# Adaptive modulation: a vector-matrix product moved from TensorE to VectorE, with one TensorE sum over partitions

## The chip, the cores and the metric

One core of a Trainium2 chip runs the whole program in one launch. The metric is the device time of a run in microseconds, as the median of several runs.

## The reference, cut to what matters

Two blocks of a network follow each other over 256 tokens of width 1024, in float32. Block one has two layers, each a mixer, a cross attention and a gated FFN (hidden width 2816). Block two is conditioned on a vector `c`: one product gives six vectors of 1024 that shift, scale and gate it.

```python
mod = jax.nn.silu(c) @ w_ada[l] + b_ada[l]        # (1, 1024) @ (1024, 6144)
shift1, scale1, gate1, shift2, scale2, gate2 = jnp.split(mod, 6, axis=-1)
h = modulate(rms_norm_2(x, norm_pre_mix[l]), shift1, scale1)
...
x = x + gate1[:, None, :] * rms_norm_2(mix @ w_out[l], norm_post_mix[l])
h2 = modulate(rms_norm_2(x, norm_pre_ffn[l]), shift2, scale2)
y = expert_choice_ffn(h2, w_router[l], w_gate[l], w_up[l], w_down[l])   # 16 experts, hidden 2816
x = x + gate2[:, None, :] * rms_norm_2(y, norm_post_ffn[l])
```

The modulation depends on `c` alone, so its 25 MB weight can be worked on at any time before block two. The 16 experts' weights are 554 MB.

## The kernel before, in words

**Weights of block one.** Dense weights come from memory in units of 1 MB (tile `raw`, three buffers). Each unit is used in two halves of 128 x 1024, and each half is split into a high float32r part by ScalarE (`wh`, L206) and the rest by VectorE (`wl`, L207). There are five buffers for halves, and a next half is split as soon as the products of an earlier one have freed its place. Every product is three TensorE products (L249 to L251).

**The second layer's FFN** (`ffn`, L886) runs through 11 groups g of 256 hidden columns, and a round here is one g: the gate's product, the up product, and the down product of group g-1. After the gate's product comes a tanh on ScalarE and `fth` on VectorE (L903); after the up product comes another `fth` (L913), which is split into `dH` on ScalarE (L289) and `dL` on VectorE (L290). The program calls `between()` after the gate's and after the down product, and each call puts in one unit of a list of fills.

**The modulation** (`ada_unit`, L987) is that list in the second layer: 24 units A0 to A23. Each has 1 MB of `w_ada` (tile `adw`, two buffers, all 1024 rows by 256 columns). TensorE multiplies it in eight products of 128x256 with `crep`, which holds silu(c) repeated 32 times (L1001); four partial sums lie 32 partitions apart in PSUM. They are split into high and low parts (`adsb`, L1007 and L1008), and one unit later two products with the selecting matrix `sel` add the four (L1015, tile `ae`); VectorE adds bias and gain (L1018 to L1021). A0 and A1 are put ahead of the transposes of the norm before the FFN (`bound`, L1073), A2 behind them, A3 to A23 into the FFN. The last sum is flushed in the first norm of block two (L1277).

**Queues.** The order is written out by hand and every engine works in the program's order. All weights are loaded through SyncE's one queue. A load whose place is still in use waits there, and every load behind it waits too.

**Memory of the experts' stage.** The pool `work` of all that comes before is released and the pool of the experts is laid over the same addresses, so an expert's load waits until the last reader of what lay in its slot has finished. From the lowest address on, `work` holds:

```python
decay = tile_(work, (P, 4, S), "decay")       # 4096 bytes of a partition
causal = tile_(work, (P, P), "causal")        # 512
cos = tile_(work, (P, 2, 32), "cos")          # 256
sin = tile_(work, (P, 2, 32), "sin")          # 256
rep8 = tile_(work, (8, P), "rep8")            # 512
identr = tile_(work, (P, 8), "identr", F32R)  # 32
crep = tile_(work, (P, KC, 32), "crep")       # 1024
hH = tile_(work, (P, KC, S), "hH", F32R)      # 8192
hL = tile_(work, (P, KC, S), "hL", F32R)      # 8192
```

Next come two tiles of 4096 bytes with the tag `gain`. Gains of the norms use them, and in the routing, the last stage before the experts, the normalised rows `h2T` (L1495), which the router's product `plg` reads (L1029). The experts have 14 slots of 2816 x 4 = 11264 bytes, placed by a list:

```python
SLOTS_AT = [1, 2, 11, 5, 3, 7, 8, 9, 12, 13, "y", "hid", "hT", "ds", "sT", "fs", 10, 0, 4, 6]
```

So slot 1 has bytes 0 to 11264 of the pool and slot 2 bytes 11264 to 22528. The first load of expert 0 goes to slot 0, the second to slot 1, the third to slot 2, and so on (`feed` in `experts`, L1622, issues at L1632 and L1635). The 15th load waits until TensorE has used the first one's slot.

Of the kernel before, what the change touches and what calls it, by code (L numbers as in the profile page):

```python
# [8 lines left out]
F32 = mybir.dt.float32  # L9
# [22 lines left out]
def shape_constants():  # L32
    """Constants that depend on shapes and positions in an array alone."""
# [16 lines left out]
    sel = np.zeros((P, P), np.float32)  # L50
    sel[0::32, :] = 1.0
    c["k_sel"] = sel
# [12 lines left out]
def log1p_coefficients(degree=9, n=200):  # L65
    """The polynomial of log(1 + y) / y through its Chebyshev nodes on [0, 1]."""
    t = np.cos(np.pi * (np.arange(n) + 0.5) / n)
    y = (t + 1) / 2
    cheb = np.polynomial.chebyshev.chebfit(t, np.log1p(y) / y, degree)
    poly = np.polynomial.Polynomial(np.polynomial.chebyshev.cheb2poly(cheb))  # L70
    return [float(v) for v in poly(np.polynomial.Polynomial([-1.0, 2.0])).coef]
# [6 lines left out]
def tile_kernel(ctx: ExitStack, tc: tile.TileContext, I, out, stop=None):  # L78
# [22 lines left out]
    # what is used up first lies lowest: the experts' weights take its place  # L101
# [6 lines left out]
    crep = tile_(work, (P, KC, 32), "crep")  # L108
# [6 lines left out]
    # the parts of what goes into a second projection; the memory holds other  # L115
    # things before
# [9 lines left out]
    # ---------------------------------------------------------------- steps  # L126
# [40 lines left out]
    def run_program():  # L167
# [7 lines left out]
        def feed():  # L175
            # the last weight has a place of its own, so that no load behind it waits
# [87 lines left out]
    def proj_n(W, o, aH, aL, t):  # L264
        """o[token, column] of a half of the tokens."""
# [26 lines left out]
    # ---------------------------------------------------------------- norms  # L292
# [39 lines left out]
    def pre_norm_b(t, xg, dg, oH, oL):  # L332
        """oH + oL = transpose of norm(src) * gain for a half of the tokens."""
# [10 lines left out]
    def post_norm_a(t, acc, gain):  # L344
# [3 lines left out]
        # one bank's squares beside the other's products  # L348
# [18 lines left out]
    # ------------------------------------------------------------ once only  # L367
# [17 lines left out]
    def prepare():  # L385
# [17 lines left out]
        # 2 softplus(-lam), and -4  # L403
# [10 lines left out]
        nc.vector.tensor_scalar(ct, ct, 0.5, None, op0=OP.mult)  # L414
        nc.vector.tensor_copy(crep, ct[:, :, None].to_broadcast([P, KC, 32]))

    # ----------------------------------------------------- memory's keys, values
# [44 lines left out]
    def mixer(l, fill, also=(lambda: None,) * 3):  # L462
# [39 lines left out]
        def fox_spread():  # L502
            # -8 times the sums, and rows of zeros below them
# [314 lines left out]
    def gelu2(o, src, pool, shape, key):  # L818
        """o = 2 gelu(src), its tanh form; src in PSUM."""
# [8 lines left out]
    # --------------------------------------------------------- cross attention  # L828
# [59 lines left out]
    # ------------------------------------------------------------------- ffn  # L888
    def ffn(l, between):
# [50 lines left out]
    # ------------------------------------------------- block two: modulation  # L940
    B = {}

    def ada_open():
# [17 lines left out]
        B["sel"] = p.tile([P, P], F32R, name="sel", tag="sel", bufs=1)  # L961
        raw = p.tile([P, 256], F32, name="selraw", tag="adb", bufs=2)[:, :P]
        nc.sync.dma_start(raw, I["k_sel"])
        ada_rest.append(lambda: nc.scalar.copy(B["sel"], raw))
# [5 lines left out]
    ADA = [(j, u) for j in (1, 0, 2, 4, 3, 5) for u in range(4)]  # L970
    ada_w = {}

    def ada_load(i):
        if i < len(ADA):
            j, u = ADA[i]
            src, shp = cols(I["w_ada_2"][0], j * D + 256 * u)
# [775 lines left out]
```

## Time and profile before

| what | us |
|---|---|
| median of 3 runs | 2388.23 |
| range of the runs | 2387.13 to 2389.67 |
| profiled execution: its span, first to last instruction (the page lists no other time of it) | 2385.8 |
| busy: TensorE / VectorE / ScalarE | 1815.9 / 747.7 / 542.2 |
| data moved | 747.16 MB, mean 313 GB/s |

The span is 2.4 us shorter than the median of the runs. Engines are named PE (TensorE products), PEld (its weight loads), DVE (VectorE), ACT (ScalarE), POOL (GpSimd) and SP (SyncE). Busy shares of the whole span mix stages that have different limits: the first 1085 us or so are dense work on TensorE, the rest is the experts. So the stages are read apart.

### The profile page before, as it was taken

The page shows a single profiled execution, that of the slowest core. Times are in us where ns is not written, and L with a number is a line of the kernel's source. Part 1 is how long each engine was busy: PE and PEld are TensorE (multiplying, and loading weights), DVE is VectorE, ACT ScalarE, POOL GpSimd, SP SyncE. Part 2 cuts the span into 40 slices and gives each one's busy share as a digit, 9 for nine tenths or more (in the row PEclk, how much of TensorE's full clock was granted, in tenths as well). Part 3 has the DMA queues.
Part 4 walks back from the last instruction along what each step waited for, and adds up shares of the span by engine and source line. Part 5 has one row for each costly group of instructions (what it writes and reads, how often), then busy time and mean ns, then how long its engine had stood idle before and what let it go on. Part 6 is the DMA issues. An engine that isn't in the chain of part 4 may idle for free.

```text
span 2385.8 us, 30667 instructions
## 1 busy us (share of the span) xinstructions
PE 1815.9 (76%) x13172; PEld 1152.7 (48%) x13172; DVE 747.7 (31%) x1147; ACT 542.2 (23%) x882; POOL 54.8 (2%) x96
## 2 busy tenths in 40 slices
PE   7999999999989999979556656655655665565565
PEld 7889899988878888964111111111111111111111
DVE  5774555557656555651000000000000000000001
ACT  4554444445444333531000000000000000000000
POOL 0010000000000000020000000000000000000000
PEclk9999999999999999979999899989999999999999
DMA  6344555453568886569999999999999999999997
GB/s 218 124 166 161 176 184 188 142 172 123 186 204 287 279 279 196 181 235 365 419 421 417 416 422 419 417 418 422 417 416 420 419 417 417 422 418 416 420 421 287
DMA packets 244423, 747.16 MB, mean 313 GB/s; under 512 B 21024, under 2 KB 151728, under 8 KB 211520
## 3 DMA queue, kind: packets, MB, share of 16 engines
q1 hardware_dynamic: 241696, 744.40, 80.7%
q8 instruction: 103, 1.69, 0.3%
q10 hardware_dynamic: 2592, 0.81, 0.1%
q14 instruction: 32, 0.26, 0.0%
HBM read 743.99 MB, written 1.05 MB: 312 GB/s over the span
## 4 chain that ended last, share of the span: by engine, by line
DMA 52%; PE 37%; DVE 5%; ACT 2%; POOL 1%; issue 1%; SPq 1%; ACTq 0%; POOLq 0%; DVEq 0%
DMA ed<-in_w_down_dram 18%; DMA eu<-in_w_up_dram 18%; DMA eg<-in_w_gate_dram 15%; PE fu L249 2%; PE fu L251 2%; PE fu L250 2%; PE fg L249 2%; PE fg L251 2%; PE fg L250 2%; PE facc L251 2%; PE facc L250 2%; PE facc L249 2%; DVE wl L207 1%; PE ad L1001 1%; PE pd L1686 1%
## 5 line engine op out<-in xcount | busy, mean ns | idle before, releaser
L207 DVE TENSOR_TENSOR wl<-raw,wh 128x1024 fp32r<-128x1024 f32 (+1 forms) x284 | 341.5, 1216 | 228.9 <-ACT wh L206 228.2
L1686 PE MATMUL pd<-ed,hT 128*32 128x512 f32 x1408 | 319.5, 617 | 93.6 <-DMA ed<-in_w_down_dram 89.0
L1659 PE MATMUL pu<-eu,xsT 128*32 128x384 f32 (+1 forms) x2048 | 205.3, 481 | 199.3 <-DMA eu<-in_w_up_dram 199.3
L1659 PE MATMUL pg<-eg,xsT 128*32 128x384 f32 (+1 forms) x2048 | 201.1, 479 | 190.8 <-DMA eg<-in_w_gate_dram 190.8
L206 ACT CAST wh<-raw 128x1024 fp32r<-128x1024 f32 (+1 forms) x284 | 292.1, 1042 | 226.7 <-PE fg L250 44.2
L1664 DVE SCALAR_TENSOR_TENSOR hid<-hid,pg 128x384 f32<-128x384 f32 (+2 forms) x48 | 19.8, 413 | 720.9 <-ACT hid L1663 720.9
L1686 PEld LDWEIGHTS pd<-ed,hT 128*32 128x32 f32 x1408 | 69.6, 111 | 331.4 <-DMA ed<-in_w_down_dram 165.2
L1659 PEld LDWEIGHTS pu<-eu,xsT 128*32 128x32 f32 x2048 | 62.1, 111 | 330.6 <-DMA eu<-in_w_up_dram 276.5
L1659 PEld LDWEIGHTS pg<-eg,xsT 128*32 128x32 f32 x2048 | 56.1, 111 | 332.2 <-DMA eg<-in_w_gate_dram 266.2
L1663 ACT ACTIVATE hid<-pg 128x384 f32<-128x384 f32 (+2 forms) x48 | 18.3, 381 | 829.9 <-PE pg L1659 773.3
L1698 DVE TENSOR_TENSOR y<-y,po 128x512 f32<-128x512 f32 x60 | 41.3, 688 | 409.9 <-PE po L1693 409.9
L249 PE MATMUL fu<-hH,wh 128*128 128x256 f32 x352 | 100.3, 285 | 0.0
L251 PE MATMUL fu<-hH,wl 128*128 128x256 f32 x352 | 100.3, 285 | 0.0
L250 PE MATMUL fu<-hL,wh 128*128 128x256 f32 x352 | 100.2, 285 | 0.0
L249 PE MATMUL fg<-hH,wh 128*128 128x256 f32 x352 | 99.6, 283 | 0.0
L1688 ACT COPY ds<-pd 128x512 f32<-128x512 f32 x16 | 9.4, 585 | 396.8 <-PE pd L1686 396.8
L250 PE MATMUL fg<-hL,wh 128*128 128x256 f32 x352 | 99.5, 283 | 0.0
L251 PE MATMUL fg<-hH,wl 128*128 128x256 f32 x352 | 99.5, 283 | 0.0
L251 PE MATMUL facc<-wh,dL 128*128 128x512 f32 x176 | 69.3, 393 | 0.0
L250 PE MATMUL facc<-wl,dH 128*128 128x512 f32 x176 | 68.9, 391 | 0.0
L249 PE MATMUL facc<-wh,dH 128*128 128x512 f32 x176 | 68.6, 390 | 0.0
L249 PEld LDWEIGHTS fu<-hH,wh 128*128 128x128 f32 x352 | 68.0, 193 | 0.0
(614 smaller groups left out, 3210.3 us busy)
## 6 DMA issues: line engine op xcount, KB each, us to landing
eg<-in_w_gate_dram SPq DMA_DIRECT2D x128, 1408.0 KB, 26.7
eu<-in_w_up_dram SPq DMA_DIRECT2D x128, 1408.0 KB, 27.1
ed<-in_w_down_dram SPq DMA_DIRECT2D x175, 1024.0 KB, 19.0
raw<-in_w_in_dram SPq DMA_DIRECT2D x31, 1024.0 KB, 5.5
adw<-in_w_ada_dram SPq DMA_DIRECT2D x24, 1024.0 KB, 8.6
raw<-in_w_gate_dram SPq DMA_DIRECT2D x22, 1024.0 KB, 5.2
raw<-in_w_up_dram SPq DMA_DIRECT2D x22, 1024.0 KB, 5.2
raw<-in_w_down_dram SPq DMA_DIRECT2D x22, 1024.0 KB, 5.2
```

What stands on the lines that cost most here:

```text
L206: nc.scalar.copy(h, v)
L207: nc.vector.tensor_tensor(l, v, h.bitcast(F32), op=OP.subtract)
L249: nc.tensor.matmul(o, aH, bH, start=first, stop=False)
L250: nc.tensor.matmul(o, aH, bL, start=False, stop=False)
L251: nc.tensor.matmul(o, aL, bH, start=False, stop=last)
L1001: nc.tensor.matmul(o[b:b + 32, :], crep[:, k, :], W[:, k, :], start=k < 4, stop=k > 3)
L1659: nc.tensor.matmul(pg[n][32 * j:32 * j + 32, b, :m * P].rearrange("p (c f) -> p c f", f=P), B["xsT"][:, k, 32 * e:32 * e + 32], w[:, c0:c0 ...
L1663: nc.scalar.activation(d, pg["g"][:np_, b, c0:c1], AF.Tanh, scale=0.5)
L1664: nc.vector.scalar_tensor_tensor(d, d, 1.0, pg["g"][:np_, b, c0:c1], op0=OP.add, op1=OP.mult)
L1686: nc.tensor.matmul(pd[n][32 * j:32 * j + 32, :], hT[:, i, 32 * j:32 * j + 32], w[:, a * D + n * 512:a * D + n * 512 + 512], start=i == 0, ...
L1688: nc.scalar.copy(ds_[:, :512], pd[0])
L1698: nc.vector.tensor_tensor(yb, yb, po, op=OP.add)
```

## The change

- `crep` becomes `csil`, one value of silu(c) a row: 32 bytes of a partition where there were 1024. All that lies above it in `work` moves down by 992 bytes.
- A unit is now half of the rows (512) by 512 columns, still 1 MB. VectorE multiplies each chunk of 128 rows by its silu(c) and adds it to an accumulator `ada` of 128x512: four instructions a unit, the very first of a pair a `tensor_scalar`, the other seven `scalar_tensor_tensor`.
- Every second unit (h = 1) splits the accumulator into high and low parts, and at the start of the next unit two TensorE products of 128x512 with a matrix of ones add over the partitions.
- No unit stands ahead of the transposes of the norm any more. A0 comes behind them, and the FFN gets two more calls of `between()`, after the up product of g = 2 and g = 4.

```diff
-    crep = tile_(work, (P, KC, 32), "crep")
+    csil = tile_(work, (P, KC), "csil")
...
-        nc.vector.tensor_scalar(ct, ct, 0.5, None, op0=OP.mult)
-        nc.vector.tensor_copy(crep, ct[:, :, None].to_broadcast([P, KC, 32]))
+        nc.vector.tensor_scalar(csil, ct, 0.5, None, op0=OP.mult)
...
                 unit("cols", cols(I["w_up"][l], 256 * g), f_up(g))
+                if g in (2, 4):
+                    between()
...
-    ADA = [(j, u) for j in (1, 0, 2, 4, 3, 5) for u in range(4)]
+    ADA = [(j, u, h) for j in (1, 0, 2, 4, 3, 5) for u in range(2) for h in range(2)]
...
+            ada_flush()
             W = ada_w.pop(i)
...
-            o = ps1(f"ad{j}_{u}", (P, 256))
-            for k in range(KC):
-                b = 32 * (k % 4)
-                nc.tensor.matmul(o[b:b + 32, :], crep[:, k, :], W[:, k, :], start=k < 4, stop=k > 3)
+            for k in range(4):
+                s = csil[:, 4 * h + k:4 * h + k + 1]
+                if h == k == 0:
+                    nc.vector.tensor_scalar(acc, W[:, k, :], s, None, op0=OP.mult)
+                else:
+                    nc.vector.scalar_tensor_tensor(acc, W[:, k, :], s, acc, op0=OP.mult, op1=OP.add)
             ada_load(i + 2)
...
+            if h == 0:
+                return
+            sb = B["ap"].tile([P, 2, 512], F32R, name=f"adsb{j}_{u}", tag="adsb", bufs=1)
+            put_hl(sb[:, 0, :], sb[:, 1, :], acc)

             def rest():
-                o2 = ps1(f"ae{j}_{u}", (P, 256))
+                o2 = ps1(f"ae{j}_{u}", (P, 512))
                 for a in range(2):
-                    nc.tensor.matmul(o2, B["sel"], sb[:, a, :], start=a == 0, stop=a == 1)
+                    nc.tensor.matmul(o2, B["ones"], sb[:, a, :], start=a == 0, stop=a == 1)
...
-        bound(f"post_cross{l}", f"pre_ffn{l}", n=(1, 1) if l == 0 else (2, 1))
+        bound(f"post_cross{l}", f"pre_ffn{l}", n=(1, 1) if l == 0 else (0, 1))
```

Two places show how the order moves. The first is SyncE's queue at the experts' first five loads, with the semaphores that each waits for (DMAHW is a transfer's, the others an engine's). Before:

```order
L1635 DMA eg_0_10499<-in_w_gate_dram 128x2816 [waits DMAHW1_49,DMAHW7_49,DVE_49,PE_49]
L1635 DMA eu_0_10501<-in_w_up_dram 128x2816 [waits PE_49]
L1635 DMA eg_1_10503<-in_w_gate_dram 128x2816 [waits DMAHW1_49,PE_49]
L1635 DMA eu_1_10505<-in_w_up_dram 128x2816 [waits DMAHW4_49,DMAHW3_49,DVE_49]
L1635 DMA eg_2_10507<-in_w_gate_dram 128x2816 [waits DVE_49,PE_49]
```

With the change:

```order
L1636 DMA eg_0_10272<-in_w_gate_dram 128x2816 [waits DMAHW2_49,DMAHW4_49,DVE_49,PE_49]
L1636 DMA eu_0_10274<-in_w_up_dram 128x2816 [waits PE_49]
L1636 DMA eg_1_10276<-in_w_gate_dram 128x2816 [waits DVE_49,DMAHW4_49,PE_49,Activation_49]
L1636 DMA eu_1_10278<-in_w_up_dram 128x2816 [waits DMAHW7_49,DMAHW6_49,DVE_49]
L1636 DMA eg_2_10280<-in_w_gate_dram 128x2816 [waits DVE_49]
```

The third load has new waits, on VectorE and ScalarE beside TensorE. The semaphore values in the built program belong to these instructions: before, the last product that reads `hL` (`zu`, L251); with the change, the copy of the routing's `tth` into `h2T` for the second half of the tokens (ScalarE) and the `plg` product that reads that tile last (TensorE).

The second place is VectorE in one round of the second FFN (g = 6), from the first unit of the round to the second. Before:

```order
L1020 TENSOR_TENSOR adb_1_8176<-ae_1_8275,adb_1_8176 128x256
L1021 SCALAR_TENSOR_TENSOR mod_6809<-adb_1_8176,mod_6809 128x256
L207 TENSOR_TENSOR wl_1_8306<-raw_8107,wh_1_8305 128x1024
L913 SCALAR_TENSOR_TENSOR fth_6_8252<-fth_6_8252,fu_6_8280 128x512
L290 TENSOR_TENSOR dL_6_8337<-fth_6_8252,dH_6_8336 128x512
L207 TENSOR_TENSOR wl_0_8341<-raw_8158,wh_0_8340 128x1024
L207 TENSOR_TENSOR wl_1_8357<-raw_8158,wh_1_8356 128x1024
L207 TENSOR_TENSOR wl_0_8375<-raw_8226,wh_0_8374 128x1024
L1008 TENSOR_TENSOR adsb_3_8391<-ad_3_8380,adsb_3_8391 128x256
L1020 TENSOR_TENSOR adb_2_8259<-ae_2_8394,adb_2_8259 128x256
```

With the change:

```order
L1019 TENSOR_TENSOR adb_0_7948<-ae_0_8125,adb_0_7948 128x512
L1020 SCALAR_TENSOR_TENSOR mod_6808<-adb_0_7948,mod_6808 128x512
L1002 TENSOR_SCALAR ada_1_8130<-adw_10_7954,csil 128x512
L1004 SCALAR_TENSOR_TENSOR ada_1_8130<-adw_10_7954,csil,ada_1_8130 128x512 x3
L204 TENSOR_TENSOR wl_1_8165<-raw_7985,wh_1_8164 128x1024
L909 SCALAR_TENSOR_TENSOR fth_6_8118<-fth_6_8118,fu_6_8139 128x512
L287 TENSOR_TENSOR dL_6_8196<-fth_6_8118,dH_6_8195 128x512
L204 TENSOR_TENSOR wl_0_8200<-raw_8036,wh_0_8199 128x1024
L204 TENSOR_TENSOR wl_1_8216<-raw_8036,wh_1_8215 128x1024
L204 TENSOR_TENSOR wl_0_8234<-raw_8092,wh_0_8233 128x1024
L1004 SCALAR_TENSOR_TENSOR ada_1_8130<-adw_11_8058,csil,ada_1_8130 128x512 x4
L287 TENSOR_TENSOR adsb_1_8243<-ada_1_8130,adsb_1_8243 128x512
```

The two units of a round had two instructions of 128x256 each; now the first has its adds of 128x512 and four passes over its weight, the second four passes and the split. The halves of weights (`wl`) and `dL` stand in the same order between them.

## Rows read from the trace of the kernel before

**Rows 1.** The page: the chain that ended last, share of the span by engine

```profile
DMA 52%; PE 37%; DVE 5%; ACT 2%; POOL 1%; issue 1%; SPq 1%; ACTq 0%; POOLq 0%; DVEq 0%
```

**Rows 2.** Stretches: length, busy us (instructions) of PE, PEld, DVE, ACT, POOL; clock, DMA share, GB/s

```profile
718.00:938.00 220.00, 218.46 (x1724) 190.92 (x1723) 125.32 (x162) 86.78 (x114) 0.00 (x0) 0.99 0.82 269
996.00:1064.60 68.60, 61.35 (x361) 54.03 (x360) 38.01 (x64) 25.16 (x53) 10.59 (x20) 0.83 0.52 197
1055.00:1060.00 5.00, 1.78 (x25) 1.23 (x24) 4.39 (x5) 2.54 (x8) 1.64 (x3) 1.00 0.77 284
1064.60:1100.00 35.40, 27.07 (x230) 16.07 (x234) 11.94 (x34) 6.75 (x10) 4.65 (x2) 0.81 0.83 332
1140.00:2300.00 1160.00, 697.77 (x5006) 189.53 (x4996) 81.53 (x182) 40.58 (x84) 0.00 (x0) 0.98 1.01 419
```

**Rows 3.** Chain of waits, 690 to 950 us: start us, us, work

```profile
749.57 1.00 PE ad L1001 x16
756.74 1.00 PE ad L1001 x16
757.74 0.43 PE ae L1015 x2
764.38 0.23 PE facc L251
769.41 1.00 PE ad L1001 x16
```

**Rows 4.** Groups of VectorE, 718 to 938 us: line, form, count | busy, mean ns | idle

```profile
L207 DVE TENSOR_TENSOR wl<-raw,wh 128x1024 fp32r<-128x1024 f32 x66 | 80.8, 1225 | 64.4 <-ACT wh L206 64.4
L1008 DVE TENSOR_TENSOR adsb<-ad,adsb 128x256 fp32r<-128x256 f32 x22 | 9.2, 417 | 0.0
L290 DVE TENSOR_TENSOR dL<-fth,dH 128x512 fp32r<-128x512 f32 x11 | 7.6, 693 | 7.5 <-ACT dH L289 7.5
L1021 DVE SCALAR_TENSOR_TENSOR mod<-adb,mod 128x256 f32<-128x256 f32 x15 | 6.4, 425 | 0.5
L1020 DVE TENSOR_TENSOR adb<-ae,adb 128x256 f32<-128x256 f32 x15 | 6.2, 415 | 0.3 <-DMA adb<-in_b_ada_dram 0.3
L1018 DVE TENSOR_TENSOR mod<-ae,adb 128x256 f32<-128x256 f32 x8 | 3.3, 414 | 0.0
```

**Rows 5.** Groups of VectorE, the whole span

```profile
L358 DVE SCALAR_TENSOR_TENSOR x<-ag,s,x 128x1024 f32<-128x1024 f32 x14 | 18.0, 1282 | 9.4 <-POOL s L314 9.4
L1438 DVE SCALAR_TENSOR_TENSOR gm<-zu,gm 128x512 f32<-128x512 f32 x2 | 1.4, 693 | 0.1
L822 DVE TENSOR_SCALAR gt<-gt 128x512 f32<-128x512 f32 x2 | 0.8, 417 | 0.0
```

**Rows 6.** ScalarE in order of time, one round of the second FFN

```profile
784.52 0.62 ACT L289 CAST dH<-fth 128x512 fp32r<-128x512 f32 x1 [2.67 <-DVE fth L913]
786.60 1.06 ACT L206 CAST wh<-raw 128x1024 fp32r<-128x1024 f32 x1 [0.50 <-PE facc L251]
```

**Rows 7.** SyncE's issues in order of time, 990 to 1092 us

```profile
996.26 0.34 SPq L1635 DMA_DIRECT2D eg<-in_w_gate_dram  x1
1008.06 0.34 SPq L1635 DMA_DIRECT2D eu<-in_w_up_dram  x1
1008.49 0.38 SPq L1635 DMA_DIRECT2D eg<-in_w_gate_dram  x1
...
1055.10 0.33 SPq L1635 DMA_DIRECT2D eu<-in_w_up_dram  x1
...
1086.57 0.33 SPq L1635 DMA_DIRECT2D eg<-in_w_gate_dram  x1
```

**Rows 8.** The routing in order of time, 1061 to 1064 us

```profile
1062.18 1.27 PE L1029 MATMUL plg<-h2T,wr 128*32 128x128 f32 x16
```

**Rows 9.** TensorE around the norm ahead of the second FFN

```profile
703.84 1.93 PE L1001 MATMUL ad<-adw,crep 128*32 128x256 f32 x32
709.64 3.75 PE L338 MATMUL pn<-dg,xg 128*128 128x128 f32 x16 [3.87 <-DVE dg L329]
```

More of the change, by code (lines that the diff above doesn't have):

```diff
@@ L49, in shape_constants @@
     c["k_dist"] = dist.reshape(2, P, S).transpose(1, 0, 2).copy().astype(np.float32)
-    sel = np.zeros((P, P), np.float32)
-    sel[0::32, :] = 1.0
-    c["k_sel"] = sel
     c["k_diag16"] = np.repeat(np.eye(16, dtype=np.float32)[:, :, None], 32, axis=2).copy()
@@ L960, in ada_open @@
         p = B["ap"] = tc.alloc_tile_pool(name="adaw", bufs=1, reuse_waits="tile")
[L961 to L964, printed above, removed]
+        B["ones"] = p.tile([P, P], F32R, name="ones", tag="ones", bufs=1)
+        nc.scalar.activation(B["ones"], ident, AF.Copy, scale=0.0, bias=1.0)
         for i in range(2):
@@ L974, in ada_load @@
         if i < len(ADA):
-            j, u = ADA[i]
-            src, shp = cols(I["w_ada_2"][0], j * D + 256 * u)
-            ada_w[i] = B["ap"].tile(list(shp), F32, name=f"adw{j}_{u}", tag="adw", bufs=2)
-            nc.sync.dma_start(ada_w[i], src)
+            j, u, h = ADA[i]
+            src = I["w_ada_2"][0][512 * h:512 * h + 512, j * D + 512 * u:j * D + 512 * u + 512]
+            ada_w[i] = B["ap"].tile([P, 4, 512], F32, name=f"adw{j}_{u}{h}", tag="adw", bufs=2)
+            nc.sync.dma_start(ada_w[i], src.rearrange("(k p) n -> p k n", p=P))
     ada_rest = []
+    ada_acc = {}
     def ada_flush():
@@ L986, in ada_unit @@
     def ada_unit(i):
-        j, u = ADA[i]
-        c = slice(u * 256, (u + 1) * 256)
+        j, u, h = ADA[i]
+        c = slice(u * 512, (u + 1) * 512)
         def fn():
+            ada_flush()
             W = ada_w.pop(i)
-            bias = B["ap"].tile([P, 256], F32, name=f"adb{j}_{u}", tag="adb", bufs=2)
-            nc.sync.dma_start(bias, I["b_ada_2"][0:1, j * D + u * 256:j * D + (u + 1) * 256].partition_broadcast(P))
-            o = ps1(f"ad{j}_{u}", (P, 256))
-            for k in range(KC):
-                b = 32 * (k % 4)
-                nc.tensor.matmul(o[b:b + 32, :], crep[:, k, :], W[:, k, :], start=k < 4, stop=k > 3)
-            ada_load(i + 2)
-            if i == 2:
-                ada_flush()
-            sb = B["ap"].tile([P, 2, 256], F32R, name=f"adsb{j}_{u}", tag="adsb", bufs=2)
-            nc.scalar.copy(sb[:, 0, :], o)
-            nc.vector.tensor_tensor(sb[:, 1, :], o, sb[:, 0, :].bitcast(F32), op=OP.subtract)
-            if i != 1:
-                ada_flush()
+            if h == 0:
+                ada_acc[0] = B["ap"].tile([P, 512], F32, name=f"ada{j}_{u}", tag="ada", bufs=2)
+                ada_acc[1] = B["ap"].tile([P, 512], F32, name=f"adb{j}_{u}", tag="adb", bufs=2)
+                nc.sync.dma_start(ada_acc[1], I["b_ada_2"][0:1, j * D + u * 512:j * D + (u + 1) * 512].partition_broadcast(P))
+            acc, bias = ada_acc[0], ada_acc[1]
+            for k in range(4):
[4 more added lines that the diff above has]
+                    nc.vector.scalar_tensor_tensor(acc, W[:, k, :], s, acc, op0=OP.mult, op1=OP.add)
+            ada_load(i + 2)
+            if h == 0:
+                return
+            sb = B["ap"].tile([P, 2, 512], F32R, name=f"adsb{j}_{u}", tag="adsb", bufs=1)
+            put_hl(sb[:, 0, :], sb[:, 1, :], acc)
             def rest():
-                o2 = ps1(f"ae{j}_{u}", (P, 256))
+                o2 = ps1(f"ae{j}_{u}", (P, 512))
                 for a in range(2):
-                    nc.tensor.matmul(o2, B["sel"], sb[:, a, :], start=a == 0, stop=a == 1)
+                    nc.tensor.matmul(o2, B["ones"], sb[:, a, :], start=a == 0, stop=a == 1)
                 dst = B["m"][j][:, c]
@@ L1181, in tile_kernel @@
         ffn(l, lambda: fill(1, "A"))
+        if l == 1 and stop is None:
+            assert not fills
         if l == 0:
```

## Prediction

> **What bounds the kernel now.** I read the chain of waits first. It is 52% DMA and 37% TensorE [rows 1]: two stages with two limits. The stretches show which is which [rows 2]. From 1140 to 2300 us the experts' weights arrive at 419 GB/s with a DMA share of 1.01, while TensorE is busy for 698 of 1160 us: the experts are limited by transfers, and the end of the run comes when their bytes have passed. From 718 to 938 us, the second layer's FFN with the modulation in it, TensorE is busy for 218.5 of 220 us and VectorE for 125.3, so TensorE sets the pace there. The two stages hang together by SyncE's queue: how soon experts' bytes can flow depends on how soon their slots come free [rows 7]. So the change has two questions: how much earlier the FFN ends (T), and whether the experts' loads still start as early relative to it (L).
>
> **TensorE's part of T.** On the chain a unit costs 1.00 us for its product and 0.43 us for the sum of the one before [rows 3]. In the FFN stand 21 units (A3 to A23): 21 x 1.43 = 30.0 us leave. What comes are 11 pairs of products of 128x512 with ones (the twelfth is flushed later). A product of 512 columns takes 0.23 us in a stream [rows 3]; a pair is 0.46 us, or 0.65 if its weight load shows; I take 0.65, so 7.2 us. TensorE alone would need 220.0 - 30.0 + 7.2 = 197.2 us: T is at most 22.8 us from the FFN.
>
> **VectorE's part of T.** Here the trace has prices for all that is added. A `scalar_tensor_tensor` of 128x512 with both sources in SBUF took 693 ns, a `tensor_scalar` of that size 417 ns, and the form with a scalar of each row and its output as a source, at 128x1024, 1282 ns [rows 5]. Each pass needs the one before it, so I add 0.03 us between them (estimate).
>
> - Leaves: 22 splits, 15 + 15 + 8 adds: 9.2 + 6.4 + 6.2 + 3.3 = 25.1 us [rows 4].
> - Comes: 84 x 0.72 = 60.5, 12 x 0.42 = 5.0, 12 splits x 0.69 = 8.3, and 18 adds of 128x512 in the FFN (two for scales and gates, one for shifts) x 0.69 = 12.4 us. Together 86.2.
> - Busy then: 125.3 - 25.1 + 86.2 = 186.4 us.
> - Waits that no backlog hides, since ScalarE has to cast between two VectorE instructions: 11 x 0.68 before `dL` [rows 4] = 7.5, the same before the 12 new splits = 8.2, and about 0.3 us before the `wl` behind each of these 23 = 6.9. Together 22.6.
>
> VectorE needs 209 us at the least, 12 more than TensorE. So the bound moves to VectorE and T is at most 11 us. Its round is longer than that sum suggests, because of one wait that the change adds on TensorE's queue: the pair with ones stands behind the gate's product and needs the split of the accumulator, and in rounds 5 to 10 the four passes of that unit stand behind the down product's end in VectorE's order (the second order excerpt). From that end: cast 1.06, `wl` 1.23, four passes 2.88, cast 0.62 [rows 6], split 0.69, some 0.4 of hand-overs: 6.9 us, while the gate's product lasts 756.74 - 749.57 - 1.43 = 5.74 us [rows 3]. TensorE, and all that is queued behind the pair, waits 1.1 us in each such round. A round becomes 5.74 + 1.1 + 0.65 + 11.24 = 18.7 us (up and down together take 769.41 - 757.74 - 0.43), against 769.41 - 749.57 = 19.84 [rows 3]. Six rounds give 6 x 1.1 = 7. Rounds 0 to 4 hold 12 of the 24 units, two of them three units each, which is about 22 us of VectorE in such a round; I count no gain there. **T from the FFN: 7 us, between -3 and 22.8.**
>
> **Ahead of it.** A0 and A1 ran in a hole of TensorE (703.8 to 709.6 us, the transposes wait for VectorE's `dg`) [rows 9]: their going gives nothing by itself. Two splits of VectorE and three casts of ScalarE leave the chain of that norm, and A2 stands no more ahead of the gate's product: +1.2 us, between 0 and 2. If the longer hole lowers the clock for longer, up to 1 us goes back. Behind the FFN the flush has adds of 128x512 instead of 128x256 on the norm's chain: 2 x (0.69 - 0.42) = -0.5 us. The bias loads and the modulation's loads stay 1 MB each on the same queue; they now wait for VectorE instead of TensorE, about one unit later, with a round of time to land. I cost them at nothing: the DMA share is 0.82 [rows 2]. **T = 7 + 1.2 - 0.5 = 7.7 us.**
>
> **L: the third load of the experts.** This is what the diff hardly shows. Ahead of `hH` lie 4096 + 512 + 256 + 256 + 512 + 32 + 1024 bytes; with `hH` and `hL` that makes 23072, the place where the `gain` tiles, later `h2T`, begin. Slot 2 ends at 22528: below it. With `csil` the 23072 becomes 22080, and slot 2 covers 448 bytes of `h2T`. The third load so waits for the routing's `plg` product over the second half of the tokens, and the first order excerpt has that wait. Before, the third load went out at 1008.49 us and the next ones soon after; now it goes out where `plg` passes the middle of its 16 rows, 1062.18 + 0.6 = 1062.8 us less T [rows 7, 8]. All behind it in SyncE's queue waits with it.
>
> The price: before, from 996 to 1064.6 us, 68.6 x 0.197 = 13.5 MB of experts had come, and from 1064.6 to 1100 us 35.4 x 0.332 = 11.8 MB, together 25.3 [rows 2]. With the change, two loads (2.9 MB) come early. The rest flows from 1064.6 on: a load issued at 1055.10 started some 1.6 us later (284 GB/s over the 5 us from 1055 is 3.4 us at 419) [rows 2, 7], hence 1062.8 + 1.8. It flows without a pause, since eleven loads queue and the 15th is free at 1086.57 as before [rows 7]: 35.4 x 0.419 = 14.8 MB. Missing at 1100 us: 25.3 - 17.7 = 7.6 MB, at 419 GB/s **18 us**. Ends: 17 if the burst runs at 430, 19 if it starts slowly. Nothing later gives it back, because transfers are the limit to the end.
>
> **The sum.** -7.7 + 18 = +10.3 us: a span of 2396.1 us, and with the 2.4 us by which the median stands above the span, **2398.5 us**. A run can tell some 0.2% (5 us) from no change.
>
> **The rivals.**
>
> 1. *VectorE's work is hidden after all* (it ends faster). If the waits of the cast and split overlap with backlog and the round falls to TensorE's 17.6 us, T is 22.8 + 0.7 = 23.5 and the time 2388.2 - 23.5 + 18 = 2382.7. For it: `wl` idles 64 us for ScalarE [rows 4], room that a backlog could fill. Against it: the sum of 209 us and the pair's wait. It decides from T = 23; between 13 and 23 the result is no change, faster than 2383.4 only above it. Chance 0.06; no change 0.18.
> 2. *The late load costs nothing*, because the experts catch up: then 2388.2 - 7.7 = 2380.5. For it: TensorE is idle 40% of that stage. Against it: 419 GB/s from 1140 to 2300 us; only TensorE could catch up, not the transfers. Chance 0.04.
> 3. *VectorE is slower than its old round*: with three units in two rounds and every pair late, T is -3 or less, 2408 and more. For it: 209 us leaves only 11 us for all waits on TensorE. Chance 0.17.
> 4. *The passes run at half rate.* Each of the 84 passes would last some 0.53 us longer (512 of the 1055 ns that 1024 elements add over an instruction's start, estimated from 693 and 1282 ns), 45 us more, so VectorE's 209 becomes 254 and T -34: 2440. Against it: 693 ns with two SBUF sources in float32 is the same as an add [rows 5]. Chance 0.02.
>
> [...]
>
> **How the numbers follow.** The forecast, T between -3 and 13, has 0.53 and lies above 2393. With rivals 3 and 4, slower by over 0.2% has 0.72; no change 0.18; faster 0.10 (rivals 1 and 2). The range leaves out most of the faster cases and rival 4, and takes in T from -3 to 20 with L from 17 to 19: 2386 to 2410.
>
> **What would show it.** Right: in the profile after, the third expert load goes out right behind the `plg` products, some 45 to 55 us behind the second, and then nothing but transfers at 419 GB/s; the FFN is 5 to 10 us shorter, VectorE busy for about 185 us of it, and TensorE waits before the `ae` products. Wrong: an FFN of under 200 us (then rival 1), a third load within 10 us of the second (then L is nothing), passes of over 1 us (rival 4), or an FFN of 220 us and more (rival 3).

## The result, and the profile after

| | before | with the change |
|---|---|---|
| median, us | 2388.25 (4 runs, 2387.13 to 2389.67) | 2411.58 (4 runs, 2409.98 to 2414.32) |
| ratio to before, 95% interval | | 1.0102 [1.0089, 1.0115] |
| span of the profiled execution, us | 2385.8 | 2409.0 |

The kernel became slower by 23.3 us. Forecast were 2398.5 us, with a range up to 2410.0: right in sign, and 13.1 us too low. The chain by engine, from the page of the kernel after:

```profile
DMA 53%; PE 32%; DVE 8%; ACT 2%; issue 2%; POOL 1%; SPq 1%; ACTq 0%; POOLq 0%; DVEq 0%
```

TensorE gave 5 points of the chain away and VectorE took 3 [rows 1]. The stretches of the kernel after (length, busy us of PE, PEld, DVE, ACT, POOL; clock, DMA share, GB/s):

```profile
718.00:938.00 220.00, 199.27 (x1344) 183.57 (x1344) 179.27 (x221) 82.16 (x100) 0.00 (x0) 0.95 0.81 271
1005.50:1070.60 65.10, 57.16 (x361) 49.66 (x360) 37.74 (x64) 25.17 (x53) 10.59 (x20) 0.90 0.14 48
1070.60:1109.50 38.90, 27.15 (x231) 14.95 (x230) 12.16 (x35) 6.82 (x10) 4.65 (x2) 0.82 1.00 420
1150.00:2300.00 1150.00, 696.73 (x4976) 188.93 (x4974) 81.57 (x182) 40.67 (x84) 0.00 (x0) 0.97 1.01 419
```

Between 718 and 938 us VectorE is busy for 179.3 us instead of 125.3, TensorE for 199.3 instead of 218.5 [rows 2]. Between 1005.5 and 1070.6 us only 48 GB/s arrive, where it was 197 in the like stretch before [rows 2]. After it the transfers run at 419 to 420 GB/s in the two stretches shown: nothing that was lost by then comes back. SyncE's issues in order of time, and the product that they wait for, in the kernel after:

```profile
1005.79 0.34 SPq L1636 DMA_DIRECT2D eg<-in_w_gate_dram  x1
1017.59 0.34 SPq L1636 DMA_DIRECT2D eu<-in_w_up_dram  x1
1068.97 0.33 SPq L1636 DMA_DIRECT2D eg<-in_w_gate_dram  x1
1069.42 0.37 SPq L1636 DMA_DIRECT2D eu<-in_w_up_dram  x1
...
1072.43 0.45 SPq L1636 DMA_DIRECT2D eu<-in_w_up_dram  x1
```

```profile
1068.22 1.27 PE L1028 MATMUL plg<-h2T,wr 128*32 128x128 f32 x16
```

The second load goes out at 1017.59 us, the third at 1068.97, behind the middle of `plg`. Seven more follow within 3.5 us, since they had queued behind it. Before, the third went out 0.43 us behind the second [rows 7]. This is step L of the prediction as it was written.

The FFN did not go as forecast. In the names that follow, `fg`, `fu` and `facc` are TensorE's products for the gate, for up and for down; `plc` is the router's product with the shift (a constant of its logits), `lcc` its copy on ScalarE, `lgc` the sum over that copy, and `modT` the transposes ahead of the router. VectorE's groups of the kernel after, 718 to 938 us (busy, mean ns of one | idle before):

```profile
L204 DVE TENSOR_TENSOR wl<-raw,wh 128x1024 fp32r<-128x1024 f32 x64 | 77.2, 1222 | 19.1 <-ACT wh L203 19.1
L1004 DVE SCALAR_TENSOR_TENSOR ada<-adw,csil,ada 128x512 f32<-128x512 f32 x80 | 60.1, 751 | 2.4
L287 DVE TENSOR_TENSOR adsb<-ada,adsb 128x512 fp32r<-128x512 f32 x11 | 7.6, 692 | 7.7 <-ACT adsb L286 7.7
L1002 DVE TENSOR_SCALAR ada<-adw,csil 128x512 f32<-128x512 f32 x12 | 5.8, 480 | 0.0
```

`wl` now idles 19.1 us for ScalarE where it was 64.4 [rows 4]: the room is used. A pass takes 751 ns, not 693, and the first one of a pair 480 ns, not 417 [rows 5]. TensorE's order in time in the kernel after, with what it waited for in brackets:

```profile
769.85 0.49 PE L1014 MATMUL ae<-adsb,ones 128*128 128x512 f32 x1 [3.89 <-ACT adsb L286]
770.58 0.79 PE L1014 MATMUL ae<-adsb,ones 128*128 128x512 f32 x1 [0.23 <-DVE adsb L287]
...
818.45 1.52 PE L1014 MATMUL ae<-adsb,ones 128*128 128x512 f32 x2 [3.27 <-ACT adsb L286]
...
858.16 0.50 PE L1014 MATMUL ae<-adsb,ones 128*128 128x512 f32 x1 [0.36 <-ACT adsb L286]
...
876.75 0.50 PE L1014 MATMUL ae<-adsb,ones 128*128 128x512 f32 x1 [0.36 <-ACT adsb L286]
...
919.50 0.61 PE L1048 MATMUL lgc<-sel,lcc 128*128 128x16 f32 x2 [5.70 <-ACT lcc L1046]
```

The rounds in between, as 858.16 to 876.75, take 18.6 us: the prediction said 18.7. Two of the larger waits (3.89 and 3.27 us) come behind the rounds with three units (groups 2 and 4). The third, 5.70 us, is at the router, and the prediction does not have it. ScalarE's order in time there:

```profile
913.30 1.04 ACT L203 CAST wh<-raw 128x1024 fp32r<-128x1024 f32 x1 [1.69 <-PE facc L248]
918.66 0.62 ACT L286 CAST adsb<-ada 128x512 fp32r<-128x512 f32 x1 [4.32 <-DVE ada L1004]
919.19 0.26 ACT L1046 COPY lcc<-plc 128x128 f32<-128x128 f32 x1
```

`plc` is done at 913.80 us, but its copy `lcc` stands on ScalarE behind the cast of the accumulator, and that waits 4.32 us for the four passes of A21. Behind two of these waits, the 3.27 and the 5.70 us, TensorE's granted clock was 0.70 over 10 us and 0.75 over 9 us, where it was 0.95 over the 220 us. The two stretches (same columns as above):

```profile
819.00:829.00 10.00, 10.00 (x56) 9.53 (x56) 8.85 (x12) 3.10 (x5) 0.00 (x0) 0.70 0.86 294
919.50:928.50 9.00, 9.00 (x57) 8.91 (x58) 2.38 (x5) 1.82 (x3) 0.00 (x0) 0.75 0.37 120
```

The gate's product behind the router takes 7.75 us (919.94 to 927.69) where 5.92 is usual. Last, VectorE's order in time at the end of the FFN:

```profile
941.71 3.11 DVE L1004 SCALAR_TENSOR_TENSOR ada<-adw,csil,ada 128x512 f32<-128x512 f32 x4
945.50 0.69 DVE L287 TENSOR_TENSOR adsb<-ada,adsb 128x512 fp32r<-128x512 f32 x1 [0.68 <-ACT adsb L286]
946.11 1.28 DVE L350 TENSOR_TENSOR ag<-facc,g_post_ffn 128x512 f32<-128x512 f32 x2
```

The last product of the FFN ends at 944.9 us, but the norm's first `ag` starts at 946.11: the four passes and the split of A23 stand ahead of it. Before, it started while the second half of the tokens was still multiplied (to 940.67):

```profile
937.96 1.29 DVE L353 TENSOR_TENSOR ag<-facc,g_post_ffn 128x512 f32<-128x512 f32 x2 [0.72 <-PE facc L251]
```

Where the two kernels stand against each other, by the order in time (us with the change less before; fg is the start of a group's gate product):

| fg 1 | fg 2 | fg 3 | fg 5 | fg 6 | fg 9 | fg 10 | end of FFN | first ag | second plg |
|---|---|---|---|---|---|---|---|---|---|
| -2.0 | -4.4 | +0.5 | -1.1 | +3.1 | -0.7 | +4.9 | +4.2 | +8.2 | +6.0 |

What plain rounds win is lost again in rounds 2, 5 and at the router, and the tail comes on top.

### The profile page after: what moved, and what is told of

The parts are those of the page before. It is cut to its first block, busy times and chain, and to the rows that moved or that the text cites. A ratio compares the mean times of both kernels' runs of the same rounds, so it can differ in the third digit from the quotient of the medians.

```text
span 2409.0 us, 29864 instructions
## 1 busy us (share of the span) xinstructions
PE 1810.6 (75%) x12764; PEld 1147.2 (48%) x12764; DVE 808.3 (34%) x1210; ACT 540.0 (22%) x870; POOL 53.9 (2%) x96
## 4 chain that ended last, share of the span: by engine, by line
DMA 53%; PE 32%; DVE 8%; ACT 2%; issue 2%; POOL 1%; SPq 1%; ACTq 0%; POOLq 0%; DVEq 0%
DMA eu<-in_w_up_dram 23%; DMA ed<-in_w_down_dram 17%; DMA eg<-in_w_gate_dram 12%; DVE wl L204 2%; PE fu L246 2%; PE fu L247 2%; PE fu L248 2%; DVE ada L1004 1%; PE facc L246 1%; PE facc L247 1%; PE facc L248 1%; PE fg L247 1%; PE fg L246 1%; PE fg L248 1%; PE pd L1687 1%
## 5 line engine op out<-in xcount | busy, mean ns | idle before, releaser
L1687 PE MATMUL pd<-ed,hT 128*32 128x512 f32 x1408 | 326.8, 624 | 95.3 <-DMA ed<-in_w_down_dram 90.9
L1665 DVE SCALAR_TENSOR_TENSOR hid<-hid,pg 128x384 f32<-128x384 f32 (+2 forms) x48 | 19.9, 414 | 731.2 <-ACT hid L1664 731.2
L247 PEld LDWEIGHTS fu<-hL,wh 128*128 128x128 f32 x352 | 69.0, 196 | 0.4
L248 PEld LDWEIGHTS fu<-hH,wl 128*128 128x128 f32 x352 | 68.9, 196 | 0.0
## 6 DMA issues: line engine op xcount, KB each, us to landing
ed<-in_w_down_dram SPq DMA_DIRECT2D x175, 1024.0 KB, 19.9
```

The costliest lines, as they stand in the source:

```text
L247: nc.tensor.matmul(o, aH, bL, start=False, stop=False)
L248: nc.tensor.matmul(o, aL, bH, start=False, stop=last)
L1665: nc.vector.scalar_tensor_tensor(d, d, 1.0, pg["g"][:np_, b, c0:c1], op0=OP.add, op1=OP.mult)
L1687: nc.tensor.matmul(pd[n][32 * j:32 * j + 32, :], hT[:, i, 32 * j:32 * j + 32], w[:, a * D + n * 512:a * D + n * 512 + 512], start=i == 0, ...
```

## The experiments

Times are medians; each run is called by a short name in bold, which the tables and later expectations use. The runs were made in four groups; the kernel before was timed with each (2388.09, 2388.26, 2386.18 and 2388.32 us), and ratios are to it. Between these groups the kernel before moved by up to 2.1 us, so where runs of two groups are compared, the difference of the ratios, times 2388 us, is given beside that of the medians if the two differ by over 0.5 us.

### The third load: 448 bytes, 416 bytes, and the kernel before with a like overlap

```diff
     csil = tile_(work, (P, KC), "csil")
+    tile_(work, (P, 112), "pad")
```

> The change with an unused tile of 448 bytes a partition behind csil: h2T begins at byte 22528 of the pool, where slot 2 ends. Theory (the change pays twice, some 17 us for the third expert load and some 6 us for a longer FFN and norm): the third load goes out within 1 to 15 us of the second again, and the time falls by 17 us from 2411.6 to 2394.5 us, between 2392 and 2397. Rival (all of the loss is the FFN's and VectorE's, the loads behind the third catch up): the load goes out early but the time stays within 3 us of 2411.6. Second rival (the late load costs the whole 23 us and the FFN's loss is hidden): 2388.

Measured (**pad448**): 2394.09 us (9 runs, 2392.07 to 2397.28), ratio 1.0028 [1.0018, 1.0039]. The same with 104 floats, 416 bytes:

> The same with 416 bytes, so that slot 2 covers the first 32 bytes of h2T. Theory (only whether slot and h2T share a byte counts): the third load waits for plg as with the change, 2411.6 us, within 2 us. Rival (the place of other tiles matters, or the share that is covered): in between, or as with 448 bytes.

Measured (**pad416**): 2409.94 us, 1.0093 [1.0076, 1.0110]. And the kernel before, with `crep` put above the other tiles, so that slot 2 covers 480 bytes of `h2T`:

```diff
-    crep = tile_(work, (P, KC, 32), "crep")
     hH = tile_(work, (P, KC, S), "hH", F32R)
...
         work.tile([P, n], dt, name=f"place_{tag}", tag=tag, bufs=bufs)
+    crep = tile_(work, (P, KC, 32), "crep")
```

> The kernel before, with crep moved behind the other tiles, so that hH, hL and the gain tiles (later h2T) lie 1024 bytes lower; nothing else is changed. Theory (the late third load costs 17 to 18 us by itself): 2388.2 + 17.5 = 2405.7 us, between 2404 and 2408, and the third load right behind plg. Rival (the load is hidden by what follows): 2388 within 3 us.

Measured (**before_low**): 2405.66 us, 1.0077 [1.0061, 1.0094]. SyncE's second and third issue with 448 bytes (and the fourth), with 416, and in the kernel before with `crep` moved:

```profile
1016.76 0.34 SPq L1637 DMA_DIRECT2D eu<-in_w_up_dram  x1
1017.20 0.38 SPq L1637 DMA_DIRECT2D eg<-in_w_gate_dram  x1
1035.07 0.33 SPq L1637 DMA_DIRECT2D eu<-in_w_up_dram  x1
```

```profile
1017.62 0.34 SPq L1637 DMA_DIRECT2D eu<-in_w_up_dram  x1
1067.24 0.33 SPq L1637 DMA_DIRECT2D eg<-in_w_gate_dram  x1
```

```profile
1007.55 0.34 SPq L1635 DMA_DIRECT2D eu<-in_w_up_dram  x1
1062.44 0.33 SPq L1635 DMA_DIRECT2D eg<-in_w_gate_dram  x1
```

The theory holds in all three. The late load costs 17.5 us with the change (2411.58 - 2394.09) and 17.6 us without it (2405.66 - 2388.09). An overlap of 32 bytes costs 15.9 us (2409.94 - 2394.09), nearly as much as one of 448, and the intervals of the two ratios overlap: with 32 bytes as with 448 the whole load went out late, at 1067.24 and 1068.97 us, 49.6 and 51.4 us behind the second. The rest of the loss is T: 2394.09 - 2388.09 = +6.0 us, where -7.7 was forecast. All further runs stand on the 448-byte version (in the last two `crep`, 1024 bytes, takes the place of the 448). TensorE's largest waits in its FFN are these (us in total, times, longest):

```profile
PE ae L1015 <- ACT adsb L287: 11.6, 9, 3.9
PE lgc L1049 <- ACT lcc L1047: 5.7, 1, 5.7
PE modT L1038 <- DVE mod L1018: 2.5, 1, 2.5
```

### The price of a pass

```diff
-                    nc.vector.scalar_tensor_tensor(acc, W[:, k, :], s, acc, op0=OP.mult, op1=OP.add)
+                    nc.vector.scalar_tensor_tensor(acc, W[:, k, :], 0.5, acc, op0=OP.mult, op1=OP.add)
```

> The 448-byte version with the constant 0.5 in the 96 passes instead of silu(c) of the row: this leaves silu(c) out. It asks why a pass took 751 ns and not the 693 ns that was forecast. Theory (the scalar read from SBUF for each row costs some 60 ns an instruction): 693 ns for a scalar_tensor_tensor, about 420 ns for a tensor_scalar, and some 3 to 6 us less time than the 448-byte version. Rival (other traffic in the FFN, loads or TensorE's reads, slows VectorE's accesses): 751 and 480 ns as before.

Measured (**imm**): 2389.27 us in one run, 4.8 less, and VectorE's groups in the FFN of that run:

```profile
L1005 DVE SCALAR_TENSOR_TENSOR ada<-adw,ada 128x512 f32<-128x512 f32 x82 | 56.7, 691 | 2.4
L1003 DVE TENSOR_SCALAR ada<-adw 128x512 f32<-128x512 f32 x12 | 5.0, 420 | 0.0
```

691 and 420 ns, where it was 751 and 480: the 60 ns are the scalar that each row reads from SBUF, not other traffic. It was to be seen in the rows of before: the form with a scalar of each row took 1282 ns for 1024 elements, a plain subtraction of that size 1225 [rows 4, 5]. The 693 ns that I took were of a form with a constant.

### The router's wait

```diff
-(ada_unit(i), i == 20 and step(router), i == 21 and step(router_w))
+(i == 21 and step(router_w), ada_unit(i), i == 20 and step(router))
```

> The 448-byte version with the constant of the logits (plc, lcc, lgc) put ahead of unit A21 instead of behind it, so that ScalarE's copy lcc does not stand behind the cast that waits for A21's four passes. Theory (one wait of TensorE there, 5.7 us before lgc, and the lower clock behind it, 2.3 us over the gate's product, are lost time on the path): 7 us less than 2394.1, 2387, between 2385 and 2389. Rival (VectorE sets the pace, so TensorE waits as long at the next ae instead): 2392 or more.

Measured (**router**): 2387.30 us (10 runs), 1.0004 [0.9992, 1.0016]: 6.8 us less, as forecast (5.7 by the ratios). The wait of TensorE is nearly gone:

```profile
914.50 0.40 PE L1049 MATMUL lgc<-sel,lcc 128*128 128x16 f32 x2 [0.77 <-ACT lcc L1047]
```

### The sum over partitions one unit later, one more unit early, and all three

```diff
         def fn():
-            ada_flush()
+            if h == 1:
+                ada_flush()
...
-            sb = B["ap"].tile([P, 2, 512], F32R, name=f"adsb{j}_{u}", tag="adsb", bufs=1)
+            sb = B["ap"].tile([P, 2, 512], F32R, name=f"adsb{j}_{u}", tag="adsb", bufs=2)
```

> The 448-byte version with the sum over partitions (the ae pair) one unit later, behind the next unit's start, with a second buffer for adsb; the router's two steps move one unit back with it. Theory A (TensorE's waits before ae are the loss): all of 11.6 us of waits, 4.8 us between the two products of a pair and 4 us of lower clock go, 2376, between 2374 and 2380. Theory B (VectorE sets the pace: its 16.5 us of work and 1.9 us of waits for casts make 18.4 of the 18.6 us of a round, and the waits before ae only show it): what VectorE sat idle in rounds 3 and 6 is gained, 4 to 10 us, 2384 to 2390, and rounds 7 to 9 still take 18.2 us or more. I hold B the likelier.

Measured (**flush**): 2384.86 us, 0.9994 [0.9980, 1.0008], 9.2 us less (8.1 by the ratios): within B's range, not A's. TensorE's waits in the FFN of this run:

```profile
PE modT L1039 <- DVE mod L1019: 7.9, 1, 7.9
PE ae L1016 <- ACT adsb L287: 2.3, 2, 1.5
PE lgc L1050 <- ACT lcc L1048: 1.2, 1, 1.2
```

The waits before `ae` fell from 11.6 to 2.3 us, and the one at `lgc` went as well, because the router's steps had moved along. But a new one came: the transposes `modT` wait 7.9 us for VectorE's adds. From one gate product to the next, groups 6, 7 and 8 took 17.5, 18.2 and 18.6 us: VectorE falls behind until its 18.6 us a round hold again. If the router's part is what the run before gave (6.8 us), the later sum alone gave about 2; no run has it alone.

```diff
-                if g in (2, 4):
+                if g in (0, 2, 4):
```

> The 448-byte version with one more unit early (after the up product of group 0), so that every later unit comes one place sooner and none stands behind the down product of group 9. Theory (A23's four passes and split stand on VectorE ahead of the norm's first product and cost about 4 us there): 4 to 6 us less than 2394.1, 2388 to 2390, with the first ag within 1.5 us of where its bank is done. The units with a split now stand behind the gate's product, so the waits before ae of 0.4 us in rounds 7 to 9 go too, but by theory B of the run before the rounds stay at 18.2 us or more. Rival (the work only moves to rounds 0 to 2, where VectorE is behind already): 2392 or more.

Measured (**tail**): 2394.71 us, 1.0030 [1.0019, 1.0040]: no gain, the rival's case, and my forecast failed. `ag` did start earlier (942.94 us, 946.20 in the 448-byte version), but the early rounds have more to do, and TensorE's waits were not less (22.9 us in all against 21.9):

```profile
PE ae L1015 <- ACT adsb L287: 10.6, 5, 4.7
PE lgc L1049 <- ACT lcc L1047: 6.1, 1, 6.1
PE modT L1038 <- DVE mod L1018: 5.2, 1, 5.2
```

The profiled execution of this run was its fastest (2392.09 us), so its span shows a gain that the median does not have, and no trace shows where the median loses it.

> The last three edits together on the 448-byte version. Theory (they are separate places): 7 + 6 + 4 = 17 us less, 2377, between 2372 and 2382. Rival (VectorE sets the pace everywhere, each edit alone shows the same slack): no better than the best of the three by more than 2 us, 2384 or more.

Measured (**all3**): 2384.30 us, 0.9986 [0.9975, 0.9998]: the rival again, no better than the later sum alone. The longest wait stands at the router still, only at its other step:

```profile
PE modT L1039 <- DVE mod L1019: 7.7, 1, 7.7
```

### Both terms that the forecast lacked, together

> The 448-byte version with both terms that the forecast of the FFN lacked taken out: the constant 0.5 in the passes (60 ns less each; this leaves silu(c) out) and the constant of the logits ahead of unit A21. Theory (two places that do not touch: VectorE sits idle 5 us at the router, so what it saves elsewhere adds): 2394.1 - 4.8 - 6.8 = 2382.5, between 2380 and 2385, which is where the forecast's T of 7.7 us stood without the late load (2380.5). Rival (both only show the same slack of VectorE): 2386 or more.

Measured (**imm_router**): 2384.09 us (10 runs, 2378.53 to 2388.21), 0.9991 [0.9980, 1.0002]. By the ratios that is 8.8 us less than the 448-byte version ((1.0028 - 0.9991) x 2388), with 11.6 as the sum of the single effects; the intervals allow both. In the profile the FFN's last product ends at 933.34 us, 7.3 us before that of the kernel before (940.67); the prediction had 7 for the FFN and 1.2 for what stands ahead. But 2.7 of the 7.3 were there at the first gate product (715.30 us against 718.03), and that start lies between 715.3 and 718.9 us in the profiles of these versions. The FFN itself took 218.0 us against 222.6, so it gained 4.6 us, not 7; round 5 still took 22.6 us, 19.9 before.

### A23 ahead of the norm

```diff
-            for k in range(4):
+            for k in range(4 if i < 23 else 0):
```

> The 448-byte version without the four passes of A23 (the lower half of the rows of the last pair is left out of gate2). Nothing else moves. Theory (these 3.1 us stand on VectorE ahead of the norm's first product, and on the path): ag starts 3.1 us earlier and the time is 2.5 to 3.5 us less than 2394.1, a ratio to before of 1.0013 to 1.0018. Rival (what follows waits for something else): ag earlier, but the ratio stays within 0.0005 of 1.0028.

Measured (**tail_out**): 2390.68 us (12 runs), 1.0014 [1.0003, 1.0025]: 3.4 us less, the theory's figure. VectorE's order in time at the end of the FFN:

```profile
940.66 0.68 DVE L288 TENSOR_TENSOR adsb<-ada,adsb 128x512 fp32r<-128x512 f32 x1
941.27 1.28 DVE L351 TENSOR_TENSOR ag<-facc,g_post_ffn 128x512 f32<-128x512 f32 x2
```

`ag` starts at 941.27 us, 4.9 us earlier than in the 448-byte version, 1.1 of it because this FFN ends that much earlier (943.85 against 944.98). So A23 does cost its 3 us there. Why the run with one more early unit keeps nothing of that in its median stays open.

### Versions that beat both

The steps of the router one unit later still:

```diff
-(i == 22 and step(router_w), ada_unit(i), i == 21 and step(router))
+(i == 22 and step(router), i == 23 and step(router_w), ada_unit(i))
```

> The version with all three edits, with the router's two steps one unit later still. In the run before, the wait at the router had moved, not gone: TensorE's transposes modT wait there for VectorE's adds, 9.24 us where they take 3.9. Theory (that wait is the loss that the three edits gave back): some 5 us less than 2384.3, 2379, between 2377 and 2381. Rival (VectorE's pace, the wait moves on again): 2383 or more.

Measured (**all3r**): 2378.04 us (8 runs), 0.9966 [0.9954, 0.9978]. 6.3 us less than all3 (4.8 by the ratios) went with the wait at `modT`; it did not move on:

```profile
PE ae L1016 <- ACT adsb L287: 5.8, 3, 3.8
PE lgc L1050 <- ACT lcc L1048: 1.9, 1, 1.9
```

Next, the low part of the split one unit later (`ada_lo()` at the start of a unit with h = 0):

```diff
-            put_hl(sb[:, 0, :], sb[:, 1, :], acc)
+            nc.scalar.copy(sb[:, 0, :], acc)
+            ada_low.append(lambda: nc.vector.tensor_tensor(sb[:, 1, :], acc, sb[:, 0, :].bitcast(F32), op=OP.subtract))
```

> The run all3r with one more edit: VectorE's low part of adsb is taken one unit later, so VectorE does not sit idle 0.69 us for ScalarE's cast in each of the 12 pairs. Theory B (VectorE still sets the pace): 8 us of idle time of VectorE go and the time falls by 3 to 8 us against all3r. Rival (TensorE sets the pace by now): within 1.5 us of all3r.

Measured (**lolate**): 2385.47 us, 0.9998 [0.9988, 1.0007], 7.4 us more than all3r, which neither theory had. VectorE saved the 8.2 us that it sat idle before the subtraction, but it sat idle before `wl` for 22.7 us instead of 6.2 (718 to 938 us). The subtraction now stands behind three `wl` of 1.2 us in its queue, and TensorE waits for it:

```profile
PE ae L1026 <- DVE adsb L1021: 17.9, 9, 4.9
PE lgc L1060 <- ACT lcc L1058: 1.2, 1, 1.2
```

Then three pairs on TensorE again:

```diff
                 s = csil[:, 4 * h + k:4 * h + k + 1]
+                if i // 2 in ON_PE:
+                    nc.tensor.matmul(acc[32 * k:32 * k + 32, :], crep[:, 4 * h + k, :], W[:, k, :], start=h == 0, stop=h == 1)
...
+    ON_PE = (3, 5, 8)
```

> The run lolate with three of the twelve pairs (3, 5 and 8) multiplied on TensorE again, as four products of 128x512 a unit with silu(c) repeated 32 times, whose place also takes the 448 bytes' role. VectorE loses 3 x 5.9 = 17.7 us of passes, TensorE gets some 3 x 2.1 = 6.4 us. Theory B: 4 to 10 us less than lolate. Rival (TensorE sets the pace): 4 to 6 us more than lolate.

Measured (**hyb3**): 2377.06 us, 0.9968 [0.9956, 0.9981], 8.4 us less than that base, as theory B had it. The same on all3r:

> The run all3r (2378.0, ratio 0.9966) with pairs 3, 5 and 8 multiplied on TensorE again, the low part not deferred. 17.7 us of passes leave VectorE, 6.4 us of products come to TensorE. Theory B (VectorE sets the pace): what all3r still loses, 7.1 us of waits before ae and at the router and some 3 us of lower clock behind them, falls by 3 to 8 us: ratio 0.993 to 0.9955. Rival (TensorE sets the pace in all3r): 4 to 6 us more, ratio 0.998 to 0.9995.

Measured (**hyb3r**): **2372.82 us** (6 runs, 2369.52 to 2376.47), 0.9944 [0.9926, 0.9962]: 15.5 us faster than the kernel before, some 38 us faster than the change, and within theory B's range. From hyb3 it differs in the low part alone, which comes a unit later there: that costs 4.2 us here too (5.7 by the ratios). TensorE's waits in its FFN:

```profile
PE ad L1008 <- DMA adw<-in_w_ada_dram: 4.3, 1, 4.3
PE lgc L1056 <- ACT lcc L1054: 1.2, 1, 1.2
```

None of them is for VectorE any more; the largest is for a weight's transfer, the other for the router's copy on ScalarE.

What these runs have in common is the sum of TensorE's waits from 715 us to the end of the FFN (all rows of the view of waits for products of the FFN and the modulation; the largest are shown above):

| run | waits of TensorE, us | median, us |
|---|---|---|
| tail | 22.9 | 2394.7 |
| pad448 | 21.9 | 2394.1 |
| tail_out | 21.1 | 2390.7 |
| lolate | 20.2 | 2385.5 |
| imm (one run) | 17.4 | 2389.3 |
| all3 | 17.3 | 2384.3 |
| router | 16.9 | 2387.3 |
| flush | 15.5 | 2384.9 |
| imm_router | 12.8 | 2384.1 |
| all3r | 11.2 | 2378.0 |
| hyb3 | 9.7 | 2377.1 |
| hyb3r | 5.5 | 2372.8 |

With lolate as the one that stands out, the order is nearly that of the times (the waits are of one profiled execution, the times medians). So these waits are what an edit should be judged by, and a wait that only moves is no gain. That VectorE's load alone sets the pace (theory B) is too simple: lolate took away a wait of VectorE's and got slower, because of where an instruction then stood in its order.

## Why the prediction was right and wrong

- **L: right.** 18 us forecast (17 to 19), 17.5 and 17.6 measured. The address sum, the new waits in the order and the price by missing bytes all held. One reading was off, without weight in the sum: before, the next load did not go out soon after the third, but 20 us behind it (1028.45 us).
- **TensorE's part of T: not what decided.** A pair with ones took 0.63 us where nothing was waited for (734.74 to 735.37), 0.65 forecast, and 1.2 us where its second product waited for the low part. With the waits gone nearly all, in hyb3r, the FFN still had the cost of three pairs on TensorE, so the floor of 197.2 us was not seen by itself.
- **VectorE's part of T: the step that failed.** The FFN was to end 8.2 us earlier (7 and 1.2 ahead of it) and ended 4.2 us later; the norm behind it, which was to lose 0.5 us, lost 4. Three things were missing. (1) "Comes: 84 x 0.72": four passes last 3.11 us, 0.78 each, because the price was taken from the row with a constant and not from the one with a scalar of each row; about 4.8 us (one run). (2) "One wait that the change adds on TensorE's queue" were two: the router's `lcc` stands behind a cast that waits for four passes; 6.8 us with the lower clock (0.75 over 9 us) behind it. (3) "Behind the FFN the flush has adds of 128x512": A23's passes and split were counted in VectorE's sum, but not among what stands ahead of `ag`; 3.4 us.
- **The size of that step.** Together 15.0 us by the runs made for each, with 13.7 to explain (-7.7 to +6.0). They need not add: (1) and (2) in one run gave 8.8 us and not 11.6, so with (3) some 12. What is left may be noise or the debt of round 5 (below), which no run takes out by itself. Some 2 us of the 8.2 at `ag` had come back by the second `plg`. VectorE's busy time came out (186.3 us from 718 to 946 us, 186.4 forecast), in part by luck: the passes alone were 68.9 us (63.1 + 5.8) and not 65.5. What the sum lacked was idle time: 41.7 us, with 22.6 counted.
- **Ahead of the FFN: about right.** 1.2 us forecast. In the one execution profiled of each kernel, the first gate product starts 1.3 us earlier than before (716.77 against 718.03 us), or 2.2 if the 0.9 us is taken off by which the product ahead of the norm ended later (704.80 against 703.91). The longer hole, for which up to 1 us was to go back, cost nothing that the trace shows: the transposes waited 5.73 us instead of 3.87 for `dg` and took 6.45 us from first to last (6.88 before), with a granted clock of 0.50 from 709 to 715 us in both kernels.
- **The wait before `ae`: right for a plain round** (18.7 us forecast, 18.6 measured; the wait ahead of the pair was some 0.5 us shorter than forecast and the pair 0.4 longer). The prediction's "I count no gain there" for rounds 0 to 4 was right as a sum (fg 5 came 1.1 us earlier than before, all of it won ahead of the FFN), but the debt of the second round with three units fell due in round 5, which I had counted among the winners: it lost 4.2 us (fg 5 to fg 6).
- **What was costed at nothing:** the bias and weight loads of the modulation cost nothing that the trace shows in the change; in hyb3r, when little else is left, a weight's transfer is a wait of 4.3 us.
- **The rivals.** Rival 3 (T of -3 or less, 2408 and more, chance 0.17) is what happened, with T = -6. Its reason, 209 us that leave little for all waits on TensorE, was right as far as the waits of 3.89 and 3.27 us behind the rounds with three units go; the pass's price, the router and A23 are not in it. Rival 1 did not come: VectorE's work was not hidden. Rival 2 is refuted by before_low: nothing catches up. Rival 4 is refuted by the passes: 691 ns with a constant, 751 with a scalar of each row, and 1282 at 1024 elements before. No run shows its half rate or the 0.53 us that it adds to a pass. That price was also mis-worked: the two rows it names give 1282 - 693 = 0.59 us for 512 elements, so some 2445 us.
- **The range** took T from -3 to 20; with T at -6 and L at 17.5 the result lay 1.6 us above it.

Open: what hyb3r would be without the unit moved early, what takes the gain out of the run tail's median, and how much of each wait's price is the lower clock behind it; no run takes the clock apart from the wait.

## What to carry to other kernels

Shrinking a tile moves everything above it. Where a later pool is laid over the same addresses, compute for its first loads whose bytes they touch: here 32 bytes of overlap cost 15.9 us and 448 bytes 17.5, since the whole load went out 49.6 and 51.4 us behind the one ahead of it, and the loads behind it in the queue later still. When work moves to an engine that others wait for, go through its order and list every short instruction that now stands behind the long ones (a copy for a router, a norm's first product, a split), because each is a wait of its own that the sum of busy times does not show. And take a price from the row with the same kinds of operands: a scalar read for each row cost 60 ns an instruction (751 against 691 ns at 128x512).

## What the runs showed of the hardware

- A `scalar_tensor_tensor` of 128x512 took 751 ns with a scalar of each row from SBUF and 691 ns with a constant; a `tensor_scalar` 480 and 420 ns. At 128x1024 the difference was 57 ns: the form with a scalar took 1282 ns and a plain subtraction 1225 [rows 4, 5], and at 128x512 such a subtraction took as long (692 ns) as the form with a constant.
- A load into a slot that shares its last 32 bytes with `h2T` went out at 1067.24 us, 49.62 us behind the load ahead of it; one that shares 448 at 1068.97, 51.38 us behind and 0.75 us after the start of `plg` (1068.22); one that shares none at 1017.20, 0.44 us behind.
- Behind waits of 3.27 and 5.70 us TensorE's granted clock was 0.70 and 0.75 over the next 10 and 9 us, and products that take 5.9 us took 8.18 (`fu`, from 819.77) and 7.75 (`fg`, from 919.94): 2.3 and 1.8 us on top of the waits themselves.
